# A mixer block in a newly searched order: convolution as fp32 products, head norm by columns, a kept row scale, two row maxima

## The chip, the core and the metric

One core of a Trainium2 chip runs the whole program. It has five engines with a queue each: TensorE (PE, with its weight loads shown as PEld), VectorE (DVE), ScalarE (ACT), GpSimd (POOL) and SyncE (SP), which issues transfers. The metric is the time of one execution on the device in microseconds, taken as the median of some runs.

## What is computed

The reference is one layer of an encoder with 512 rows of 1024 columns, in fp32. Three sublayers follow one another; each normalizes the rows, scales and shifts them by factors made from a second input, applies its function, normalizes the result and adds it, gated, to the running rows.

```python
def sublayer(h_res, j, fn, res_w):
    h = rms_norm(h_res, norm_g[l, 2 * j]) * (1.0 + scale) + shift
    y = rms_norm(fn(h), norm_g[l, 2 * j + 1])
    return h_res + res_w * gate * y
...
x = sublayer(x, 0, lambda h: swiglu(h, ffn1_w_in[l], ffn1_w_out[l]), 0.5)
x = sublayer(x, 1, mixer, 1.0)
x = sublayer(x, 2, lambda h: swiglu(h, ffn2_w_in[l], ffn2_w_out[l]), 0.5)
```

The change lies in the middle one. The mixer projects its 1024 columns to q, k, v, a recurrent branch xr and a gate branch yr, each 512 wide. q, k and v go through differential attention with four heads: two softmaxes per head, the second subtracted with a factor, then a norm over the head's 128 columns. xr goes through a convolution over time with four taps per channel, then through two recurrences, forward and backward, each with two gates; their sum is multiplied with GeLU of yr. Both halves are joined and projected.

```python
xc = lax.conv_general_dilated(xr, conv_w[:, None, :], window_strides=(1,), padding=[CONV_PAD],
        dimension_numbers=('NWC', 'WIO', 'NWC'), feature_group_count=D_LRU) + conv_b
h = rg_lru(xc, w_gate[0], b_gate[0], lam[0], False) + rg_lru(xc, w_gate[1], b_gate[1], lam[1], True)
...
p = jax.nn.softmax(s, axis=-1)
w = p[:, :, 0] - lam * p[:, :, 1]
...
o = rms_norm(o, subln_g) * (1.0 - lambda_init)
```

## The kernel before

Everything lies transposed: a tile has 128 channels on its partitions and the 512 rows along its free dimension, so X, the running rows, is eight such tiles. A large product is made in three fp32r products (mm3, L153 to L155): each factor is split into a high and a low part, and high x high, low x high and high x low are summed in PSUM. Weights come in units of up to 128x1024: SyncE loads one (wdma), ScalarE copies its high part (L182), VectorE or GpSimd subtracts to get the low part (L190). PSUM has eight banks of 128x512; bank() takes the one that was freed first.

The mixer (from about 405 to 630 us) is a list of small steps, MIXER, which a loop in mixer() runs through once while the program is built. Each name is a step and its argument: "sc.2" the scores of block 2. A suffix p puts it on GpSimd, d on VectorE. The list sets the order in which each engine's queue holds its instructions. Each engine works through its own queue in order; between engines, a step waits for the data and the buffers that it needs. The steps that the change and the prediction touch:

- kk, gm: the last units of the first seven column groups (four of xr, q and k of head 0, q of head 1), still on rows that are scaled but not normalized; sd, sr, rv: the norm (L994, L1001, L1004). xs, xa, rs, ra (L1041, L1049, L1106) then apply the norm to those groups.
- hm, hf, hh, hl (L1008 to L1019): the normalized columns, split high and low, for all later projections. pj: a projection, in two halves of four column tiles; vp: one of eight steps of v; vh, vl: v's parts.
- cv (L1269, L1273): the convolution of one of four groups of 128 channels on VectorE, one scaling and three multiply-adds with shifted columns; ch, cl (L1281, L959): its high and low part. ga: the two gates' products of one group and direction; gs (L1305): their sigmoids; le, lq, lr, lg, lm (L1312 to L1335): decay and input of the recurrence; ls (L1343): its scan; la (L1347), lf (L1366), lh, ll: sum of directions, times GeLU, split.
- rd, rp (L1122 to L1124): the rotary turn of q or k, three GpSimd operations; zA, zC (L1130, L1136): its split.
- sc (L1162): scores of one of 16 blocks (four heads, four blocks of 128 queries), both softmaxes side by side in two banks; mx (L1169): one operation takes the negated row maxima of both banks; ex (L1175): exponentials with row sums; wr, w1, w2 (L1180, L1184, L1188): the two softmaxes scaled and subtracted; tp, th, tl (L1199, L1209, L959): transposed and split.
- pv: weights times v; po: its copy and square; ms, me, sq, rc, mu (L1233, L1237, L1241, L1244, L1248): the norm over a head's columns, made as a full 128x512 tile: a product with ones that sums and spreads, times 1/128 plus epsilon, square root, reciprocal, product; ah, al (L1253, L1257): split.
- mo, mp: the output product, by unit of rows and by column tile; pf, pa (L1411, L1412, L1417): scaling and sum of squares for the norm that follows.

Around the mixer, X is kept with a row factor. When a sublayer's result F has its row norms s1 (a root of mean squares), half() and begin() set X to X x s1 + F (L418 to L422, L453) rather than dividing F. X is thus the true rows times s1, and the next norm's epsilon is scaled by s1 squared. To go on, the mixer divides X by it again: rr takes the reciprocal of s1 (L1425) and rx multiplies each of the eight tiles by it on GpSimd (L1428). last_tile() makes the last column tile of a result in two halves of 256 rows and the row norms after each (L899, L903, L904).

Of the kernel before, what the change touches and what calls it, by code (L numbers as in the profile page):

```python
# [81 lines left out]
ra.q2 vl.1 ex.3 wr.2 rd.q2 rx.3 lq.21 sc.0 ex.1 pj.k2a wr.3 w1.2 qkfree.0 mx.0 w1.3 ws.12 rx.6 wr.1 w2.2 ex.0
pj.k2b wl.12 w1.1 rxfree rp.q2 le.11 w2.1 wd.15 w2.3 sc.7 wr.0 ra.k2 lq.11 pj.q3a ws.13 rd.k2 mx.7 le.10 w1.0
wl.13 pj.q3b ex.7 w2.0 wd.16 lq.10 zA.q2 zC.q2 zF.q2 gs.30 sc.4 rp.k2 ga.31 mx.4 ws.14 gwfree tp.0 tp.2 wr.7 ra.q3 wl.14 tp.1
th.0 rd.q3 pj.k3a th.1 w1.7 zA.k2 th.2 lg.30 gs.31 w2.7 tl.2 zC.k2.p tp.3 tl.0 wd.17 sc.5 tl.1 th.3 sc.6
mx.5 ex.4 pj.k3b rp.q3 qkfree.1 zF.k2 tl.3 mx.6 ex.5 sc.9 wr.4 ra.k3 sc.8 wr.5 ex.6 mx.9 w1.4 rd.k3 sc.11 w1.5
pv.0 ws.15 w2.4 lg.31 w2.5 ex.9 wr.6 wl.15.p zA.q3 zC.q3 zF.q3 le.30 tp.4 tp.5 pj.y1a wr.9 w1.6 mx.8 wd.18 po.0 rp.k3 th.4
w2.6 ex.8 pj.y1b tl.4 mx.11 th.5 lr.10 tl.5 ms.0 w1.9 wr.8 lq.30 tp.7 w1.8 lr.11 w2.9 pj.y0a lm.10.p th.7 zA.k3
lr.30 w2.8 lr.21 lm.11.p tl.7 sc.10 ls.10 zC.k3.p yo.1 tp.6 ls.11 ex.11 qkfree.2 pj.y0b mx.10 lm.30 la.1
zF.k3 me.0 th.6 sc.14 ws.16 wr.11 lm.21.p tl.6 sc.15 mx.14 yo.0 pj.y2a wl.16.p ex.10 ls.21 ex.14 ls.30 wr.10 sc.12  # L90
w1.11 mx.15 wd.19 le.31 w1.10 sc.13 la.2 pv.1 wr.14 qkfree.3 mx.13 ex.15 w1.14 w2.11 ex.13 w2.14 tp.8 pj.y3a mx.12
# [1496 lines left out]
```

## Time and profile before

| | us |
|---|---|
| median of 3 runs (lowest, highest) | 1029.3 (1026.26, 1029.37) |
| the profiled execution | 1029.16 |
| its span, first to last instruction | 1027.0 |
| VectorE busy from 405 to 430 us | 24.97 of 25 |
| TensorE busy from 440 to 489 us | 38.80 of 49 |

The profile is of one execution. Its rows name an engine, the line of the kernel, the operation, output and inputs by the program's names (s and q are buffers of 128x512 and 128x4x512, PS is PSUM, wh and wl a weight's parts). An fp32r operand is shown as f32 for matmuls. Ends of matmuls are modelled and overlap; the time from one start to the next is what a matmul costs in a row of them.

### The profile page before, as it was taken

What the parts mean: (1) busy time and instruction counts of PE and PEld (TensorE: products, weight loads), DVE (VectorE), ACT (ScalarE), POOL (GpSimd) and SP (SyncE); (2) the same over time, 40 slices, a digit from 0 to 9 for tenths busy, and PEclk for the clock granted to TensorE, in tenths of its full rate; (3) what the DMA queues carried; (4) which work ended last, traced back from release to release, by engine and by line L of the source; (5) the groups of instructions that cost most, each with busy time, mean ns of one, the idle gap of its engine ahead of it and who ended that gap; (6) DMA issues with size and microseconds to landing.
All of it is one profiled execution on the core that took longest, in us unless ns stands there. A gap on an engine that the chain in (4) does not pass through costs nothing.

```text
span 1027.0 us, 11660 instructions
## 1 busy us (share of the span) xinstructions
PE 966.7 (94%) x4448; PEld 791.3 (77%) x4448; DVE 630.2 (61%) x730; ACT 429.4 (42%) x650; POOL 302.2 (29%) x218
## 2 busy tenths in 40 slices
PE   6999999999999998887888999989999999999994
PEld 4888888888888887665566788778888888888884
DVE  7967655556676649999788864887333333322226
ACT  6652233334222326566686953554322332222230
POOL 1008100000010136887887756562300000000114
PEclk9999999999999999988899999989999999999998
DMA  8745555554778642221220141223332233333312
GB/s 329 288 151 208 207 203 186 194 201 179 263 260 281 225 123 76 95 87 51 82 62 11 32 138 55 75 82 103 103 103 90 95 103 99 85 102 90 101 37 83
DMA packets 45002, 137.10 MB, mean 133 GB/s; under 512 B 7185, under 2 KB 9745, under 8 KB 44946
## 3 DMA queue, kind: packets, MB, share of 16 engines
q1 hardware_dynamic: 44082, 135.62, 39.9%
q8 instruction: 35, 0.57, 0.2%
q10 hardware_dynamic: 864, 0.74, 0.2%
q14 instruction: 21, 0.17, 0.0%
HBM read 132.14 MB, written 2.10 MB: 131 GB/s over the span
## 4 chain that ended last, share of the span: by engine, by line
PE 77%; DVE 15%; issue 3%; POOL 2%; ACT 2%; DMA 1%; SPq 0%; DVEq 0%; ACTq 0%; POOLq 0%
PE PS L154 25%; PE PS L153 25%; PE PS L155 25%; DVE wl L190 2%; DVE s L1273 2%; PE PS L1162 1%; DVE s L412 1%; DVE s L959 1%; PE PS L1199 1%; PE PS L700 1%; DVE sm L1169 1%; POOL s L524 1%; DMA q<-in_w_ada 1%; DVE X L453 1%; DVE X L422 1%
## 5 line engine op out<-in xcount | busy, mean ns | idle before, releaser
L153 PE MATMUL PS<-s,wh 128*128 128x512 f32 (+1 forms) x1032 | 397.2, 385 | 3.2 <-DVE sm L1169 1.7
L155 PE MATMUL PS<-s,wh 128*128 128x512 f32 (+1 forms) x1032 | 394.5, 382 | 5.7 <-DVE s L959 2.5
L154 PE MATMUL PS<-s,wl 128*128 128x512 f32 (+1 forms) x1032 | 394.3, 382 | 3.5 <-POOL wl L190 2.1
L190 DVE TENSOR_TENSOR wl<-st,wh 128x1024 fp32r<-128x1024 f32 (+2 forms) x149 | 192.6, 1295 | 216.8 <-ACT wh L182 216.7
L155 PEld LDWEIGHTS PS<-s,wh 128*128 128x128 f32 x1032 | 195.4, 189 | 44.5 <-DVE s L959 2.9
L153 PEld LDWEIGHTS PS<-s,wh 128*128 128x128 f32 x1032 | 195.3, 189 | 44.1 <-DVE sm L1169 2.1
L154 PEld LDWEIGHTS PS<-s,wl 128*128 128x128 f32 x1032 | 195.5, 189 | 41.4 <-POOL wl L190 2.4
L182 ACT ACTIVATE wh<-st 128x1024 fp32r<-128x1024 f32 (+2 forms) x170 | 169.9, 1001 | 130.6 <-PE PS L155 109.8
L877 POOL TENSOR_TENSOR s<-s,s 128x512 f32<-128x512 f32 x12 | 16.3, 1356 | 402.7 <-ACT s L873 402.7
L153 PE MATMUL PS<-q,wh 128*128 128x512 f32 (+1 forms) x288 | 106.9, 371 | 0.0
L154 PE MATMUL PS<-q,wl 128*128 128x512 f32 (+1 forms) x288 | 106.1, 368 | 0.0
L155 PE MATMUL PS<-q,wh 128*128 128x512 f32 (+1 forms) x288 | 106.1, 368 | 0.0
L235 DVE CUSTOM_DVE_ANT_0 q<-q,q 128x1024 bf16<-128x1024 f32 x72 | 89.8, 1247 | 0.1
L791 DVE TENSOR_TENSOR s<-s,PS 128x512 f32<-128x512 f32 x41 | 28.1, 686 | 63.9 <-PE PS L155 63.2
L786 ACT ACTIVATE s<-PS 128x512 f32<-128x512 f32 x40 | 23.9, 596 | 99.9 <-PE PS L155 99.8
L154 PEld LDWEIGHTS PS<-q,wl 128*128 128x128 f32 x288 | 54.2, 188 | 10.0 <-issue 0.2
L153 PEld LDWEIGHTS PS<-q,wh 128*128 128x128 f32 x288 | 54.3, 188 | 9.9 <-issue 0.2
L155 PEld LDWEIGHTS PS<-q,wh 128*128 128x128 f32 x288 | 54.2, 188 | 9.6
L748 ACT ACTIVATE q<-s 128x512 fp32r<-128x512 f32 x28 | 17.7, 632 | 95.9 <-DVE s L791 94.5
L190 POOL TENSOR_TENSOR wl<-st,wh 128x1024 fp32r<-128x1024 f32 (+2 forms) x20 | 41.6, 2082 | 33.6 <-ACT wh L182 32.1
L748 ACT ACTIVATE s<-s 128x512 fp32r<-128x512 f32 x16 | 10.1, 632 | 70.5 <-DVE s L791 70.5
L749 DVE TENSOR_TENSOR q<-s,q 128x512 fp32r<-128x512 f32 x28 | 22.2, 792 | 20.0 <-ACT q L748 20.0
(229 smaller groups left out, 1035.5 us busy)
## 6 DMA issues: line engine op xcount, KB each, us to landing
q<-in_w_ada SPq DMA_DIRECT2D x72, 512.0 KB, 3.8
st<-in_w2b SPq DMA_DIRECT2D x37, 512.0 KB, 3.3
st<-in_w1b SPq DMA_DIRECT2D x36, 512.0 KB, 4.5
st<-in_w1o SPq DMA_DIRECT2D x16, 512.0 KB, 4.5
st<-in_w2o SPq DMA_DIRECT2D x16, 512.0 KB, 3.6
st<-in_wma SPq DMA_DIRECT2D x16, 448.0 KB, 3.9
st<-in_w2a SPq DMA_DIRECT2D x16, 448.0 KB, 3.4
st<-in_wmb SPq DMA_DIRECT2D x9, 512.0 KB, 3.3
```

The lines of the kernel that those rows point to most:

```text
L153: PE.matmul(o, wh, ah, start=start, stop=False)
L154: PE.matmul(o, wl, ah, start=False, stop=False)
L155: PE.matmul(o, wh, al, start=False, stop=stop)
L182: ACT.activation(h[:, :n], staged[i][:, :n], AF.Copy)
L190: eng.tensor_tensor(out=l[:, :n], in0=st[:, :n], in1=h[:, :n].bitcast(F32), op=ALU.subtract)
L235: DVE.tensor_tensor_reduce(out=junk, in0=t, in1=cond, op0=ALU.mult, op1=ALU.add, scale=1.0, scalar=0.0, accum_out=ada[:, i:i + 1])
L748: ACT.activation(h, t, AF.Copy)
L749: DVE.tensor_tensor(out=l, in0=t, in1=f32(h), op=ALU.subtract)
L786: ACT.activation(t, PS[:, b], AF.Silu)
L791: DVE.tensor_tensor(out=g, in0=g, in1=PS[:, b], op=ALU.mult)
L877: POOL.tensor_tensor(out=st["acc"], in0=st["acc"], in1=t, op=ALU.add)
L1273: DVE.scalar_tensor_tensor(out=o[:, t0:t1], in0=XR[:, i, t0 + d:t1 + d], scalar=cw(q), in1=o[:, t0:t1], op0=ALU.mult, op1=ALU.add)
```

## The change

The step list is replaced by another, found by a new search over orders and engines, with new steps in it:

- Convolution: dd builds on ScalarE, for a group of channels, four diagonal 128x128 matrices with the taps, by scaling the identity with a column. cv is now four fp32 products on TensorE, of a diagonal matrix with the shifted columns, summed in one bank. ce adds the bias and copies the result on ScalarE; ch and cl read the bank directly.
- Head norm: ms takes the sums with four products that have two columns each, me is a square root of 128x8 numbers on ScalarE, rc the reciprocal of these. dx scales the identity with them, into four diagonal matrices; rb multiplies ones with these, which spreads the factors over a bank; mu multiplies with that bank on VectorE.
- X keeps its scale: rx is gone. last_tile() multiplies each half's new row norms with the old reciprocal (one VectorE operation of 128x256), and half() uses that product as X's factor.
- Two row maxima per block (mx), one for each bank, and the two banks of a block are no longer sorted.
- rp is cut into r1, r2 and r3, and r1 to r3, w1, lg, la and pa can be on either engine.

```diff
+            if "old" in st:
+                DVE.tensor_tensor(out=st["old"][:, c], in0=s1[:, c], in1=st["old"][:, c], op=ALU.mult)
...
-            b = sb[n] = sorted((bank(), bank()))
+            b = sb[n] = (bank(), bank())
...
-            a, b = sb[n]
-            DVE.tensor_reduce(out=sm[:, n, 0:2], in_=PS[:, a:b + 1:b - a], axis=AX.X, op=ALU.max, negate=True)
+            for m in range(2):
+                DVE.tensor_reduce(out=sm[:, n, m:m + 1], in_=PS[:, sb[n][m]], axis=AX.X, op=ALU.max, negate=True)
...
+            b = O["m", h] = bank()
+            for q in range(4):
+                PE.matmul(PS[:, b, 2 * q:2 * q + 2], O[h][1][:, q * 128:q * 128 + 128], ones[:, 0:2], start=True, stop=True)
...
+            ACT.activation(rm[:, h], PS[:, b, 0:8], AF.Sqrt, scale=1.0 / 128, bias=epsc[:, 0:1])
...
+            DVE.reciprocal(rm[:, h], rm[:, h])
...
+            for q in range(4):
+                ACT.activation(t[:, q * 128:q * 128 + 128], ident, AF.Copy, scale=rm[:, h, 2 * q:2 * q + 1])
...
-            DVE.reciprocal(O[h][1], O[h][1])
...
+            DVE.tensor_tensor(out=o, in0=o, in1=PS[:, b], op=ALU.mult)
...
+            for q in range(4):
+                ACT.activation(dg[i][:, q * 128:q * 128 + 128], ident, AF.Copy,
+                               scale=par[:, C_CW + 4 * q + i:C_CW + 4 * q + i + 1])
...
-            for q, d in ((0, -2), (1, -1), (3, 1)):
+            for q, d in ((2, 0), (0, -2), (1, -1), (3, 1)):
                 t0, t1 = max(0, -d), min(S, S - d)
-                DVE.scalar_tensor_tensor(out=o[:, t0:t1], in0=XR[:, i, t0 + d:t1 + d], scalar=cw(q), in1=o[:, t0:t1],
-                                         op0=ALU.mult, op1=ALU.add)
+                PE.matmul(PS[:, b, t0:t1], dg[i][:, q * 128:q * 128 + 128], XR[:, i, t0 + d:t1 + d],
+                          start=d == 0, stop=q == 3)
...
-        def rx(e, k):
-            POOL.tensor_tensor(out=X[:, k], in0=X[:, k], in1=s1, op=ALU.mult)
...
-            return lambda st, c: G.half(st["F"], st["s1"], c)
+            return lambda st, c: G.half(st["F"], st.get("old", st["s1"]), c)
```

Of the list itself, the place of the first score block shows how far it is turned over: before, all of v's steps stand ahead of sc.2; now it comes after the first half of the k projection.

```diff
-lg.10 lm.20 zF.k0 rsfree gs.21 ls.01 rx.0 wl.10 ga.11 ws.11 la.0 ls.20 pj.q2a wd.13 vh.0 wl.11 gs.11 lg.21 vl.0
-vh.2 wd.14 vh.3 lg.11 sc.2 vl.2 vh.1 vl.3 le.21 sc.3 rx.2 mx.2 sc.1 rx.5 pj.q2b mx.3 rx.4 ex.2 mx.1 rx.1 ga.30
+ga.21 lg.01 cl.3 zC.q0 zF.q0 gs.21 ga.11 zC.k0 zF.k0 hl.1.p gs.11 pj.k1a sc.2 mx.2 gs.10 hl.7.p ce.3 le.00
+lq.00 pj.k1b ws.7 lg.10.p sc.0 ex.2 vp.0a mx.0 r2.q1.p ra.k1 wl.6.p vp.1a wl.7 le.10 rd.k1 r2.k1 r1.k1 lq.10
```

Three places of the engines' queues follow, each before and after; new lines of the kernel have other numbers (L959 is L965, L1004 is L1010, L1008 is L1014). A number behind a buffer's letter tells one use from another.

VectorE at the mixer's start, before: s_2635 is s1, s_2849 the mixer's norm.

```order
L190 TENSOR_TENSOR wl<-st,wh 128x896 x2
L1425 RECIPROCAL s_2635<-s_2635 128x512
L994 SCALAR_TENSOR_TENSOR s_2849<-PS,s_2848 128x512
L959 TENSOR_TENSOR q_3054<-q_81,q_3053 128x1024
L1004 RECIPROCAL s_2849<-s_2849 128x512
L1008 TENSOR_TENSOR s_3144<-X,s_2849 128x512
L1008 TENSOR_TENSOR s_3146<-X,s_2849 128x512
L1008 TENSOR_TENSOR s_3153<-X,s_2849 128x512
```

And now:

```order
L193 TENSOR_TENSOR wl<-st,wh 128x896 x2
L1000 SCALAR_TENSOR_TENSOR s_2849<-PS,s_2848 128x512
L1010 RECIPROCAL s_2849<-s_2849 128x512
L193 TENSOR_TENSOR wl<-st,wh 128x896
L1014 TENSOR_TENSOR s_3094<-X,s_2849 128x512
L193 TENSOR_TENSOR wl<-st,wh 128x896
L1014 TENSOR_TENSOR s_3147<-X,s_2849 128x512
L1021 TENSOR_SCALAR s_3158<-s_3158,aA,ada 128x512
```

The reciprocal of s1 and the split of the gates' weights (q_3054) no longer stand between the two weight splits and the norm; the reciprocal comes 43 rows later.

TensorE behind the last product of the column groups (s_2982, s_2983), before; s_3176 and the others are normalized columns.

```order
L153 MATMUL PS<-s_2982,wh 128x512
L154 MATMUL PS<-s_2982,wl 128x512
L155 MATMUL PS<-s_2983,wh 128x512
L153 MATMUL PS<-s_3176,wh 128x512
L154 MATMUL PS<-s_3176,wl 128x512
L155 MATMUL PS<-s_3177,wh 128x512
L153 MATMUL PS<-s_3169,wh 128x512
L154 MATMUL PS<-s_3169,wl 128x512
L155 MATMUL PS<-s_3170,wh 128x512
L153 MATMUL PS<-s_3164,wh 128x512
L154 MATMUL PS<-s_3164,wl 128x512
L155 MATMUL PS<-s_3165,wh 128x512
```

And now, where L1302 is the convolution, q_3055 is xr, s_3153, s_3142 and s_3189 are the diagonal matrices, s_3253 and s_3254 the convolved group's parts, q_3053 the gates' weights.

```order
L1302 MATMUL PS<-q_3055,s_3153 128x512
L1302 MATMUL PS<-q_3055,s_3153 128x510
L1302 MATMUL PS<-q_3055,s_3153 128x511 x2
L156 MATMUL PS<-s_2982,wh 128x512
L157 MATMUL PS<-s_2982,wl 128x512
L158 MATMUL PS<-s_2983,wh 128x512
L1302 MATMUL PS<-q_3055,s_3142 128x512
L1302 MATMUL PS<-q_3055,s_3142 128x510
L1302 MATMUL PS<-q_3055,s_3142 128x511 x2
L1302 MATMUL PS<-q_3055,s_3189 128x512
L1302 MATMUL PS<-q_3055,s_3189 128x510
L1302 MATMUL PS<-q_3055,s_3189 128x511 x2
```

The first half of the k projection has left this place, and three of the four convolutions stand in it, of which one comes ahead of the last column group.

VectorE behind the first two convolutions, before: s_3325 is the third convolution, q_3052 q of head 0.

```order
L190 TENSOR_TENSOR wl<-st,wh 128x1024
L959 TENSOR_TENSOR s_3282<-s_3247,s_3281 128x512
L959 TENSOR_TENSOR s_3286<-s_3252,s_3285 128x512
L190 TENSOR_TENSOR wl<-st,wh 128x1024
L1041 TENSOR_TENSOR s_3321<-PS,s_2849 128x512
L1269 TENSOR_SCALAR s_3325<-q_3055,par 128x512
L1273 SCALAR_TENSOR_TENSOR s_3325<-q_3055,par,s_3325 128x510
L1273 SCALAR_TENSOR_TENSOR s_3325<-q_3055,par,s_3325 128x511 x2
L1136 SCALAR_TENSOR_TENSOR s_3366<-q_3052,s_3365 128x512
L959 TENSOR_TENSOR s_3370<-s_3325,s_3369 128x512
```

And now, behind the low part of the first group (L1321 is cl, L1132 and L1136 are two thirds of the rotary turn, L1366 is lg):

```order
L965 TENSOR_TENSOR s_3248<-s_3202,s_3247 128x512
L1132 TENSOR_TENSOR q_3052<-q_3052,sinT 128x512
L193 TENSOR_TENSOR wl<-st,wh 128x1024
L1321 SCALAR_TENSOR_TENSOR s_3240<-PS,par,s_3239 128x512
L1321 SCALAR_TENSOR_TENSOR s_3300<-PS,par,s_3299 128x512
L1136 TENSOR_TENSOR q_3052<-q_3052 128x512
L1021 TENSOR_SCALAR s_3234<-s_3234,aA,ada 128x512
L1136 TENSOR_TENSOR q_3052<-q_3052 128x512
L1366 TENSOR_TENSOR q_3288<-q_3288,s_3322 128x512
L965 TENSOR_TENSOR s_3225<-s_3147,s_3224 128x512
L1366 TENSOR_TENSOR q_3288<-q_3288,s_3282 128x512
L1366 TENSOR_TENSOR q_3306<-q_3306,s_3282 128x512
```

The convolution is gone from this place; rotary operations and lg, which GpSimd had, stand there, and behind these rows follow the low part of the fourth group, the splits of head 0's q and k, and the first row maxima.

More of the change, by code (lines that the diff above doesn't have):

```diff
@@ L82 @@
[L82 to L91, printed above, removed]
@@ L1118, in rd, with r1, r2, r3 @@
                 SP.dma_start(out=rot[32 * q:32 * q + 32], in_=t[32 * p:32 * p + 32])
-        def rp(e, key):
+        def r1(e, key):
             t, rot = rp_[key]
-            POOL.tensor_tensor(out=t, in0=t, in1=cosT, op=ALU.mult)
-            POOL.tensor_tensor(out=rot, in0=rot, in1=sinT, op=ALU.mult)
-            POOL.tensor_tensor(out=t, in0=t, in1=rot, op=ALU.add)
+            e.tensor_tensor(out=t, in0=t, in1=cosT, op=ALU.mult)
+        def r2(e, key):
+            t, rot = rp_[key]
+            e.tensor_tensor(out=rot, in0=rot, in1=sinT, op=ALU.mult)
+        def r3(e, key):
+            t, rot = rp_[key]
+            e.tensor_tensor(out=t, in0=t, in1=rot, op=ALU.add)
         def zA(e, key):
@@ L1183, in w1 @@
             p = P[n][1]
-            POOL.tensor_scalar(out=p, in0=p, scalar1=sm[:, n, 7:8], scalar2=lamc[:, 4:5], op0=ALU.mult, op1=ALU.mult)
+            e.tensor_scalar(out=p, in0=p, scalar1=sm[:, n, 7:8], scalar2=lamc[:, 4:5], op0=ALU.mult, op1=ALU.mult)
         def w2(e, n):
@@ L1264, in mixer, with dd, ce @@
         am = {}
[L1266 to L1274 removed]
+        dg, cb = {}, {}
+        def dd(e, i):
+            dg[i] = ar.s()
+            for q in range(4):
+                ACT.activation(dg[i][:, q * 128:q * 128 + 128], ident, AF.Copy,
+                               scale=par[:, C_CW + 4 * q + i:C_CW + 4 * q + i + 1])
+        def cv(e, i):
+            b = cb[i] = bank()
+            for q, d in ((2, 0), (0, -2), (1, -1), (3, 1)):
+                t0, t1 = max(0, -d), min(S, S - d)
+                PE.matmul(PS[:, b, t0:t1], dg[i][:, q * 128:q * 128 + 128], XR[:, i, t0 + d:t1 + d],
+                          start=d == 0, stop=q == 3)
+            ar.give(dg.pop(i))
+        def ce(e, i):
+            xc[i] = ar.s()
+            b = cb.pop(i)
+            ACT.activation(xc[i], PS[:, b], AF.Identity, bias=par[:, C_CB + i:C_CB + i + 1])
+            unbank(b)
         def xrfree(e):
@@ L1280, in ch @@
             xch[i] = (ar.s(F32R), ar.s(F32R))
-            ACT.activation(xch[i][0], xc[i], AF.Copy)
+            ACT.activation(xch[i][0], PS[:, cb[i]], AF.Identity, bias=par[:, C_CB + i:C_CB + i + 1])
         def cl(e, i):
-            low(e, xch[i][1], xc[i], xch[i][0])
+            b = cb[i]
+            DVE.scalar_tensor_tensor(out=xch[i][1], in0=PS[:, b], scalar=par[:, C_CB + i:C_CB + i + 1],
+                                     in1=f32(xch[i][0]), op0=ALU.add, op1=ALU.subtract)
         def ga(e, k):
@@ L1327, in lg @@
             g = RI[d, 1][:, i]
-            POOL.tensor_tensor(out=g, in0=g, in1=xc[i], op=ALU.mult)
+            e.tensor_tensor(out=g, in0=g, in1=xc[i], op=ALU.mult)
             if d == 1:
@@ L1346, in la @@
             o = RI[1, 1][:, i]
-            POOL.tensor_tensor(out=o, in0=o, in1=RI[0, 1][:, i], op=ALU.add)
+            e.tensor_tensor(out=o, in0=o, in1=RI[0, 1][:, i], op=ALU.add)
         def rifree(e):
@@ L1416, in pa @@
             t = sqs.pop(m)
-            POOL.tensor_tensor(out=st["acc"], in0=st["acc"], in1=t, op=ALU.add)
+            e.tensor_tensor(out=st["acc"], in0=st["acc"], in1=t, op=ALU.add)
             ar.give(t)
@@ L1452, in part @@
                 mm3(PS[:, b, c], w[0][:, o], w[1][:, o], a[0][:, c], a[1][:, c], k == 0, k == 7)
+        st["old"] = s1
         last_tile(1, st, part, 4, nxt, early)
@@ L1504, in trunk_kernel @@
         G.begin(st["F"], st["s1"])
+        ar.give(st["old"])
         G.rest(2)
```

71 lines of the change are left out of this document (40 added, 31 removed).

## Prediction

> **What bounds the kernel now.** I read the page first, for the engines' totals.
>
> ```profile
> span 1027.0 us, 11660 instructions
> PE 966.7 (94%) x4448; PEld 791.3 (77%) x4448; DVE 630.2 (61%) x730; ACT 429.4 (42%) x650; POOL 302.2 (29%) x218
> ```
>
> TensorE is busy 94% of the span, and the two SwiGLUs on either side of the mixer hardly ever let it wait. So only the mixer is open, from 405 us (the last weights before its norm) to 630 us (its last products). The windows of that stretch are the second view; columns: length, then busy time and instructions of PE, PEld, DVE, ACT and POOL, then the granted clock.
>
> ```profile
> 405.00:430.00 25.00, 22.42 (x95) 17.25 (x93) 24.97 (x19) 13.95 (x19) 20.78 (x11) 1.00 0.31 104
> 430.00:440.00 10.00, 4.75 (x15) 3.08 (x16) 9.82 (x10) 6.95 (x12) 8.71 (x7) 0.88 0.12 26
> 440.00:489.00 49.00, 38.80 (x152) 30.64 (x151) 48.75 (x33) 32.67 (x48) 40.08 (x24) 0.88 0.26 75
> 489.00:566.00 77.00, 65.71 (x314) 47.28 (x312) 62.55 (x69) 56.02 (x109) 61.30 (x44) 0.96 0.17 48
> 566.00:630.00 64.00, 63.99 (x297) 51.95 (x298) 40.33 (x37) 43.72 (x77) 42.46 (x30) 0.97 0.27 83
> ```
>
> From 405 to 489 VectorE is never free and TensorE stands still for 2.58 + 5.25 + 10.20 us. From 489 to 566 TensorE stands still for another 11.29 us, and from 566 it has no gap at all. That is 29.3 us of waits. The clock loses more: (1 - clock) x busy time is 0.57, 4.66, 2.63 and 1.92 us in the last four windows, 9.8 us. Waits and clock together are **39.1 us**: all that any order of the mixer can win while TensorE does the same work.
>
> Third, TensorE's timeline, for what the larger gaps wait on (the bracket is the gap and its releaser).
>
> ```profile
> 430.33 0.50 PE L155 MATMUL PS<-s,wh 128*128 128x512 f32 x1 [1.05 <-POOL s L959]
> 437.58 0.74 PE L153 MATMUL PS<-s,q 128*128 128x512 f32 x1 [4.69 <-ACT s L1281]
> 478.47 0.80 PE L155 MATMUL PS<-wl,s 128*128 128x512 f32 x1 [5.48 <-DVE wl L190]
> 491.95 1.82 PE L1162 MATMUL PS<-s,s 64*128 64x512 f32 x7 [1.57 <-DVE q L959]
> 494.67 1.64 PE L1162 MATMUL PS<-s,s 64*128 64x512 f32 x5 [0.90 <-DVE sm L1169]
> ```
>
> The first gap is the k projection waiting for a normed column. The second is the gates waiting for the convolution (L1281 splits its result, L1273 makes it); the third is V's product waiting for a weight split that stands in VectorE's queue; the last two are scores behind evictions and row maxima.
>
> Why VectorE is full is in its rows by line, min/median/max in ns:
>
> ```profile
> L959 DVE TENSOR_TENSOR s<-s,s x7: 679/1749/1781, 426.0 to 474.5; 128x512 fp32r<-128x512 f32 x7
> L959 DVE TENSOR_TENSOR q<-PS,q x20: 666/678/692, 491.2 to 587.5; 128x512 fp32r<-128x512 f32 x20
> L1273 DVE SCALAR_TENSOR_TENSOR s<-q,par,s x12: 750/1659/2778, 431.9 to 464.4; 128x511 f32<-128x511 f32 x8, 128x510 f32<-128x510 f32 x4
> L1428 POOL TENSOR_TENSOR X<-X,s x8: 1251/1276/1727, 474.0 to 503.7; 128x512 f32<-128x512 f32 x8
> ```
>
> An operation with both operands in SBUF takes 0.68 us alone and 1.75 us while POOL works, POOL's own goes from 1.28 to 1.73, and with one operand in PSUM nothing slows it. So each POOL operation that meets VectorE costs VectorE about 1.07 us. The other two large kinds that stay on VectorE, alone and, for the first, beside POOL:
>
> ```profile
> 480.02 2.30 DVE L190 TENSOR_TENSOR wl<-st,wh 128x1024 fp32r<-128x1024 f32 x1
> 608.42 1.23 DVE L190 TENSOR_TENSOR wl<-st,wh 128x1024 fp32r<-128x1024 f32 x1 [0.60 <-ACT wh L182]
> 482.25 1.21 DVE L1343 TENSOR_TENSOR_SCAN q<-q,q 128x512 f32<-128x512 f32 x1
> L1169 DVE TENSOR_REDUCE sm<-PS 128x2 f32<-128x1024 f32 x16 | 19.5, 1220 | 10.9 <-PE PS L1162 4.3 <-PE PS L155 3.3 <-ACT s L1175 2.7
> ```
>
> The split of 608.42 is VectorE's last large one in the mixer; the last line is the row maxima.
>
> **The change, part by part.** *Convolution on TensorE.* Removed from VectorE, with the four other large operations that the head norm loses:
>
> ```profile
> L1273 DVE SCALAR_TENSOR_TENSOR s<-q,par,s 128x511 f32<-128x511 f32 (+1 forms) x12 | 19.2, 1599 | 0.4
> L1269 DVE TENSOR_SCALAR s<-q,par 128x512 f32<-128x512 f32 x4 | 3.0, 750 | 0.0
> L1244 DVE RECIPROCAL s<-s 128x512 f32<-128x512 f32 x4 | 13.2, 3327 | 0.3 <-ACT s L1241 0.3
> L1237 DVE TENSOR_SCALAR s<-PS 128x512 f32<-128x512 f32 x4 | 2.7, 677 | 1.2 <-PE PS L1233 1.2
> ```
>
> 38.1 us leave VectorE. On TensorE 16 fp32 products appear. The trace has such products in the old head norm; start to start one takes 544.47 - 543.61 = 0.86 us (two instructions), where an fp32r product takes 0.23.
>
> ```profile
> 543.15 0.39 PE L154 MATMUL PS<-s,wl 128*128 128x512 f32 x1
> 543.38 0.39 PE L155 MATMUL PS<-s,wh 128*128 128x512 f32 x1
> 543.61 1.02 PE L1233 MATMUL PS<-s,ones 128*128 128x512 f32 x2
> 544.47 0.60 PE L1199 MATMUL PS<-ident,s 128*128 128x128 f32 x4
> 394.64 1.62 PE L395 MATMUL PS<-ones,s 128*128 128x2 f32 x14
> ```
>
> 16 x 0.86 = **13.8 us**, all on TensorE, which is the engine that ends last. Bounds: 0.23 x 16 = 3.7 us if they ran like fp32r; above, at half clock, twice 0.86, 27.5 us. I take 13.8, the same form's own row.
>
> *Head norm by columns.* Its full-width product stays (now it spreads the factor); 16 products with two columns are new, at 1.62 / 14 = 0.116 us: **+1.9 us** on TensorE. Six operations in a chain replace five, and at the last head TensorE has two slices of the output product (24 x 0.23 = 5.5 us) to work on meanwhile, so I give the latency nothing. Uncovered, it would gain at most the old reciprocal's 3.3 us, or lose at most the two new links, four scalings of 0.36 us (below) and a product of 0.86.
>
> *ScalarE* gets 32 scalings of 128x128 with a column, four more evictions and two more table loads.
>
> ```profile
> L1412 ACT ACTIVATE s<-PS,aG x7: 678/682/718, 608.8 to 627.1; 128x512 f32<-128x512 f32 x7
> L894 ACT ACTIVATE s<-PS,aG x6: 460/467/468, 372.8 to 1012.6; 128x256 f32<-128x256 f32 x6
> L1313 ACT ACT_TABLE_LOAD x2 | 2.6, 1283 | 0.0
> ```
>
> Carried on in a straight line, 128 columns take 0.467 - 0.215 / 2 = 0.36 us, so 32 take 11.5 us, with the rest about 15 us, onto 153 us of 225. That is hidden except between convolution and gates (below). *Two maxima per block* instead of one of 1.22 us cost VectorE 16 x 0.14 us more, by the 0.68 us of an operation on one bank of PSUM; in return the first exponential starts 0.6 us earlier. I call it even.
>
> *X keeps its scale.* Eight POOL operations (L1428, 10.9 us with the mean 1.38) go, and so does the need for the 3.34 us reciprocal to run first:
>
> ```profile
> 410.45 3.34 DVE L1425 RECIPROCAL s<-s 128x512 f32<-128x512 f32 x1
> 413.71 0.62 DVE L994 SCALAR_TENSOR_TENSOR s<-PS,s 128x512 f32<-128x512 f32 x1
> 414.25 2.41 DVE L959 TENSOR_TENSOR q<-q,q 128x1024 fp32r<-128x1024 f32 x1
> 416.59 3.34 DVE L1004 RECIPROCAL s<-s 128x512 f32<-128x512 f32 x1
> ```
>
> The mixer's own reciprocal (L1004) now follows the statistics directly: it ends at about 415.1 instead of 419.9, 4.8 us earlier. TensorE has products until 428 either way, so this buys nothing by itself, but the normed columns are ready in time. Against it, one 128x256 product on VectorE stands in each half of the last norm's chain:
>
> ```profile
> L420 DVE TENSOR_TENSOR X<-X,s x8: 426/693/968, 376.8 to 638.3; 128x256 f32<-128x256 f32 x8
> ```
>
> 0.43 us with POOL idle, which here waits for the same product; behind it in VectorE's queue stand the products on X and the next weights' activations, for which TensorE waits. That is 0.4 to 0.9 us for both halves, and I take **+0.7**.
>
> *The new order.* I follow the engines' orders from 428 us with the durations above. TensorE: first convolution at 427.8, two more until 438.9, two gate pairs until 441.7. The next pair waits for a split that stands behind three two-operand operations on VectorE (1.7, 1.7 and 2.2 us, from 437.5): it starts at 443.8, **2.1 us** lost. The fourth convolution and three pairs end at 453.2, half of the k projection at 455.9. Then the first score block needs head 0's k, seven such operations later on VectorE, at about 459: **3.1 us** lost. V's eight steps (12 x 0.23 each) and three more score blocks end at 487 us. Before, V ended at 489 with half a q projection (2.7 us) done and no score block; now four blocks (3.5 us) are done. The front thus keeps 2.6 us of waits for the statistics, 5.2 us of these two, and at the clock of 0.88 for some 10 us another 1.2: **9.0** of its 23.3 us.
>
> For the attention part (15.8 us of waits and clock now) the two quoted waits of 1.57 and 0.90 us and 1.4 us of slow clock behind them go, since those blocks now run beside V's products, and so does L1237's (0.76 us). Of the 11.2 us left I keep **7.0**: VectorE's load there hardly falls (twelve scalings and half of the rope come over from POOL, the reciprocals go), so by kind these waits stay.
>
> [...] After the waits of 1.57 and 0.90 us the chain shows products 0.43 us apart, half speed:
>
> ```profile
> 497.03 0.43 PE PS L154
> 497.46 0.43 PE PS L155
> ```
>
> [...]
>
> **The sum.** 39.1 - 13.8 - 1.9 - 9.0 - 7.0 = 7.4 us saved, 0.7 given back: 6.7. The profiled execution took 1029.16 us (span 1027.0 us and 2.2 around it), 0.1 below the median of 1029.3, so I forecast **1022.5 us**. Its own range: if the remaining 16 us of waits are off by 6 either way, 1016.5 to 1028.5. As a check from VectorE: from 437 us on it keeps 64 two-operand operations at 0.65, eight scans and ten splits at 1.2, and some 49 us of the rest, 111 us; POOL's 52 operations add 1.07 each if all of them meet it (55 us), 33 if six in ten do. 144 us at the share that it reached before (152.5 us busy of 172.6 up to its last split) take 163 us: VectorE is done at 600, and 21.5 us later, as now, the mixer at 622. The first sum says 623.
>
> **The rivals.** *TensorE becomes the only bound.* The waits vanish but for the first 2.6: 39.1 - 15.7 - 2.6 - 0.7 = 20.1, so 1009; with a few left, 1012. For it speaks the last window, 64 us without a gap; against it, that two engines would be over 85% busy and hand work to each other. Chance 0.20.
>
> *The waits move.* The gate pairs need PSUM banks that only ScalarE's sigmoids free, and V's fourth bank comes from the first exponential; by my count that ends at 463.1 and V starts at 463.5. ScalarE has some 60 instructions between 416 and 455 there, 16 of 0.36 and the rest of about L1412's 0.68 us, 35 us in all. Should it run 7 us late, V starts 7 us late and the gain is gone: 1029. Chance 0.12. What speaks for it: its queue holds evictions behind copies that wait for VectorE, in order.
>
> *Slower: VectorE is slowed by POOL throughout.* The moved operations are two-operand ones. If nearly all of POOL's 52 operations meet them (45 to 55 us instead of 33), VectorE needs 156 to 166 us, 177 to 189 at its share, is done at 614 to 626, and the mixer ends at 636 to 647: 1035 to 1046. It decides from about 40 us of collisions. For it: L959's median of 1.75 us, near its maximum; against: fewer POOL operations are left to collide. Chance 0.13, at 1036.
>
> That the convolution wouldn't move can be left out: the order shows its products on TensorE.
>
> **How the numbers follow.** 0.55 for the forecast, 0.20, 0.12 and 0.13 for the rivals. Some 0.3% (3.1 us) is what a measurement of this kernel can tell from no change, so faster is below 1026. The forecast's own range lies nine tenths below it, 0.50, and the first rival adds 0.20, with a small part of the second: 0.72. Same: 0.05 and most of the second, 0.14. Slower 0.14. The range leaves out the far end of either rival: 1009 to 1032.
>
> **What would show it.** Right: the granted clock near 0.95 or more from 430 to 489; the fp32 products 0.86 us apart; TensorE's gaps at the third gate pair and at the first score block on VectorE, 2 and 3 us; V finished near 487; gaps of about 7 us afterwards. Wrong: two-operand operations on VectorE whose median stays at 1.7 us; a gap ahead of V that ends with an exponential or a sigmoid; fp32 products dearer than 0.86 us, which all falls on the end.

## The result and the profile after

The changed kernel took 1011.34 us (median of 4 runs, 1010.0 to 1013.34), the kernel before 1028.08 us beside it: ratio 0.984, 95% interval 0.9814 to 0.9866. That is 16.7 us less, where 6.7 were forecast; direction and range held, the size was off by 10. The profiled execution took 1012.05 us, 17.1 less than the profiled one of before. Its page:

```profile
span 1010.1 us, 11805 instructions
PE 973.8 (96%) x4512; PEld 796.6 (79%) x4512; DVE 598.1 (59%) x766; ACT 440.9 (44%) x687; POOL 238.9 (24%) x173
```

TensorE has more to do (973.8 us for 966.7) and the program is shorter. The mixer as one window shows why. Its last norm's first product comes at 611.72 us, where it came at 629.99. Columns: length, then busy time of PE, PEld, DVE, ACT and POOL, then the clock. First before, then after:

```profile
405.00:630.00 225.00, 195.67 (x868) 150.19 (x867) 186.42 (x164) 153.30 (x261) 173.33 (x113) 0.95 0.23 69
```

```profile
405.00:612.00 207.00, 201.61 (x932) 153.89 (x931) 155.71 (x198) 164.85 (x298) 110.14 (x68) 1.00 0.24 75
```

TensorE's waits fall from 29.3 to 5.4 us and its granted clock goes from 0.95 to 1.00. The work can be checked here: 195.67, less the 9.8 us that the slow clock had taken, plus 13.8 for the convolution and 1.9 for the head norm, is 201.6, as measured. GpSimd has 63 us less to do, VectorE 31. By stage, after:

```profile
428.00:440.00 12.00, 12.00 (x33) 5.93 (x33) 7.90 (x10) 10.30 (x17) 7.49 (x5) 1.00 0.36 101
440.00:487.00 47.00, 45.21 (x196) 33.40 (x195) 37.15 (x42) 44.53 (x72) 30.11 (x18) 1.00 0.27 87
487.00:550.00 63.00, 61.26 (x319) 49.03 (x317) 57.73 (x85) 53.06 (x99) 33.59 (x21) 1.00 0.22 67
550.00:612.00 62.00, 62.00 (x302) 49.00 (x301) 32.52 (x50) 42.55 (x85) 21.94 (x16) 1.00 0.27 81
612.00:645.00 33.00, 29.10 (x171) 25.17 (x170) 27.70 (x31) 15.28 (x26) 21.59 (x19) 0.95 0.14 42
```

TensorE is the only bound now, although VectorE is busy 57.7 of 63 us beside it in the third row. All waits of TensorE of 0.4 us or more that are left up to 620 us, in its timeline after, with the convolutions (L1302), the first score block (L1174) and the start of the last norm (L902):

```profile
407.61 1.12 PE L472 MATMUL PS<-s,ones 128*128 128x512 f32 x2 [1.85 <-POOL s L468]
...
427.84 3.59 PE L1302 MATMUL PS<-q,s 128*128 128x512 f32 x8
431.96 7.01 PE L1302 MATMUL PS<-q,s 128*128 128x512 f32 x16
443.39 0.50 PE L158 MATMUL PS<-s,q 128*128 128x512 f32 x1 [1.23 <-DVE s L1321]
445.17 3.69 PE L1302 MATMUL PS<-q,s 128*128 128x512 f32 x8 [0.56 <-ACT q L1343]
455.60 0.96 PE L1174 MATMUL PS<-s,s 64*128 64x512 f32 x6
...
493.24 0.50 PE L156 MATMUL PS<-s,wh 128*128 128x512 f32 x1 [0.46 <-ACT s L1116]
503.21 0.50 PE L156 MATMUL PS<-s,wh 128*128 128x512 f32 x1 [1.28 <-DVE q L965]
...
611.72 0.59 PE L902 MATMUL PS<-s,ones 128*128 128x256 f32 x2
616.51 0.39 PE L156 MATMUL PS<-s,wh 128*128 128x256 f32 x1 [1.21 <-ACT s L412]
617.70 0.39 PE L158 MATMUL PS<-s,wh 128*128 128x256 f32 x1 [0.69 <-DVE s L415]
```

The first score block starts without a wait at 455.6; the forecast had it behind 3.1 us of waiting, at 459. Its reason is on VectorE, in the rows that lead to that block:

```profile
446.93 1.76 DVE L1136 TENSOR_TENSOR q<-q 128x512 f32<-128x512 f32 x1
448.62 0.68 DVE L1366 TENSOR_TENSOR q<-q,s 128x512 f32<-128x512 f32 x1
449.22 0.68 DVE L965 TENSOR_TENSOR s<-s,s 128x512 fp32r<-128x512 f32 x1
...
453.78 0.68 DVE L965 TENSOR_TENSOR s<-q,s 128x512 fp32r<-128x512 f32 x1
```

From 448 us on they take 0.68 us, since GpSimd waits just there, for ScalarE (L1025, and L1343 after that):

```profile
443.77 4.37 POOL L965 TENSOR_TENSOR s<-s,s 128x512 fp32r<-128x512 f32 x3
450.76 1.29 POOL L965 TENSOR_TENSOR s<-s,s 128x512 fp32r<-128x512 f32 x1 [2.62 <-ACT s L1025]
455.90 1.29 POOL L1366 TENSOR_TENSOR q<-q,s 128x512 f32<-128x512 f32 x1 [3.85 <-ACT q L1343]
```

### The profile page after: what moved, and what is told of

Same layout as the page of the kernel before. It is cut to its first block, busy times and chain, and to the rows that moved or that the text cites. A ratio compares the mean times of both kernels' runs of the same rounds, so it can differ in the third digit from the quotient of the medians.

```text
span 1010.1 us, 11805 instructions
## 1 busy us (share of the span) xinstructions
PE 973.8 (96%) x4512; PEld 796.6 (79%) x4512; DVE 598.1 (59%) x766; ACT 440.9 (44%) x687; POOL 238.9 (24%) x173
## 4 chain that ended last, share of the span: by engine, by line
PE 86%; DVE 6%; ACT 3%; POOL 2%; issue 2%; DMA 1%; SPq 1%; DVEq 0%; ACTq 0%; POOLq 0%
PE PS L156 27%; PE PS L157 27%; PE PS L158 27%; PE PS L1174 1%; DVE wl L193 1%; DVE s L415 1%; PE PS L703 1%; PE PS L1211 1%; POOL s L527 1%; DVE X L456 1%; DVE X L425 1%; DMA q<-in_w_ada 1%; DVE s L1549 1%; POOL s L468 1%; DVE X L423 1%
## 5 line engine op out<-in xcount | busy, mean ns | idle before, releaser
L193 DVE TENSOR_TENSOR wl<-st,wh 128x1024 fp32r<-128x1024 f32 (+3 forms) x150 | 190.5, 1272 | 226.7 <-ACT wh L185 226.6
L156 PEld LDWEIGHTS PS<-q,wh 128*128 128x128 f32 x288 | 54.3, 189 | 10.2 <-issue 0.6
L193 POOL TENSOR_TENSOR wl<-st,wh 128x1024 fp32r<-128x1024 f32 (+1 forms) x19 | 38.4, 2020 | 55.3 <-ACT wh L185 50.4
```

Of the source, the lines that this page charges most:

```text
L156: PE.matmul(o, wh, ah, start=start, stop=False)
L193: eng.tensor_tensor(out=l[:, :n], in0=st[:, :n], in1=h[:, :n].bitcast(F32), op=ALU.subtract)
```

## Experiments

Two questions: which bound the changed kernel has, and where the forecast's waits went. All ratios are to the kernel before on the same chip, which took 1026.3 to 1027.2 us there; the changed kernel stands at 0.984, some 1010 us. A price below is the difference of two ratios times 1027 us, good to about 3 us. In the profiled executions some of that lies ahead of every edit: the mixer's first wait ends between 407.6 and 409.3 us. Most of these kernels have the step list on one line, so their lines are numbered 29 or 30 lower: L936 or L935 is L965, L1145 is L1174, L1273 is L1302.

**All four convolutions back on VectorE**, in the new list:

```diff
+            if i in {0, 1, 2, 3}:
+                o = xc[i] = ar.s()
...
+                for q, d in ((0, -2), (1, -1), (3, 1)):
+                    t0, t1 = max(0, -d), min(S, S - d)
+                    DVE.scalar_tensor_tensor(out=o[:, t0:t1], in0=XR[:, i, t0 + d:t1 + d], scalar=cw(q), in1=o[:, t0:t1],
+                                             op0=ALU.mult, op1=ALU.add)
+                return
```

> The changed kernel with all four convolutions back on VectorE, at the same places of the new list (no diagonal matrices, no fp32 products, the bias in VectorE's first scaling; the split reads SBUF again). TensorE loses 13.8 us of products, VectorE gets back some 22 us (19.2 + 3.0 by the rows of before) between 428 and 450 us. Theory relief (the waits went because VectorE lost work; the products are cheaper than the waits that they remove): the gates wait for VectorE again, 4 to 6 us a group at first, and the time is 1013 to 1025 us in spite of 13.8 us less on TensorE. Theory order (the new list removes the waits by itself, the move of the convolution is a cost): 998 to 1003 us.

1025.07 us, ratio 0.9989 (0.9977 to 1.0001): the whole gain is gone. TensorE in its front:

```profile
446.06 0.80 PE L156 MATMUL PS<-s,q 128*128 128x512 f32 x1 [15.82 <-ACT s L1331]
455.59 0.80 PE L158 MATMUL PS<-s,q 128*128 128x512 f32 x1 [4.16 <-DVE s L965]
466.59 0.50 PE L156 MATMUL PS<-s,wh 128*128 128x512 f32 x1 [3.48 <-ACT q L1362]
```

It has 13.8 us less to do and stands still for 23.5; its clock of 0.71 from 428 to 440 us and 0.78 from there to 487 costs another 8.0. The relief of VectorE in the front is what this order lives on.

**One convolution back on VectorE**, the fourth group's, by the same edit for that group:

> The changed kernel with only the last convolution (group 3) on VectorE, which has some 10 of 47 us free there now. If TensorE alone is the bound: 3.4 us less, 1008 us. If VectorE's front is as full as the prediction had it: the first score block waits 3 to 6 us longer for head 0's split, and the time is 1011 to 1015 us.

1014.78 us, 0.9886 (0.9871 to 0.9901), 4.7 us more. The time is as the second theory had it, but the wait stands at another place: at the gates' products, ahead of the first score block. L1331 is ScalarE's copy of the convolved group, L1362 the gates' sigmoids:

```profile
452.74 0.63 ACT L1331 ACTIVATE s<-s 128x512 fp32r<-128x512 f32 x1 [3.94 <-DVE s L1307]
455.03 0.80 PE L156 MATMUL PS<-s,q 128*128 128x512 f32 x1 [5.11 <-ACT q L1362]
```

VectorE isn't full: it is busy 36.0 us from 440 to 487, and the convolution's four operations take 2.9. It is done late (452.7 us), since it stands behind other work in VectorE's queue; ScalarE's sigmoids stand behind its copy, and TensorE behind them.

**Each convolution made twice** on TensorE:

```diff
-            for q, d in ((2, 0), (0, -2), (1, -1), (3, 1)):
+            for _ in range(2):
+                for q, d in ((2, 0), (0, -2), (1, -1), (3, 1)):
...
```

> The changed kernel with each convolution made twice into the same bank (the second pass overwrites the first): 16 more fp32 products, 13.8 us more on TensorE and nothing else. If TensorE alone bounds the mixer now: 12 to 14 us more, 1023.5 to 1025.5. If VectorE or ScalarE hold the front as well, part of it disappears in waits that were there: less than 10 us more, under 1021.

1021.42 us, 0.9953 (0.9939 to 0.9968): 16 products more cost 11.6 us of their 13.8, and of the waits of 1.23 and 0.56 us behind them 0.25 is left. TensorE is the bound: what it gets to do falls on the end, less the small waits that it fills.

**The new steps in the old list**, on the engines that the old steps had, each put where its old step stood (the convolution right ahead of its split); one piece of the list:

```diff
-wl.5 hh.6 hl.4.p ch.2 ga.01 gs.00 hl.6 wd.8 cl.2 rp.q0 pj.k1b wl.6 gs.01 rs.q1 wd.9
+wl.5 hh.6 hl.4.p cv.2 ch.2 cl.2 ce.2 ga.01 gs.00 hl.6 wd.8 r1.q0.p r2.q0.p r3.q0.p pj.k1b wl.6 gs.01 rs.q1 wd.9
```

> The new steps (convolution on TensorE, head norm by columns, two maxima, kept scale with its late reciprocal) in the list of before, with each new step put beside the one that it belongs to and the old engines kept for the rope, w1, lg, la and pa. Theory relief: most of the gain without the new list, 1012 to 1019 us. Theory order: the new steps alone only add 15.7 us to TensorE in a list that was made for others, 1026 to 1036 us.

1026.8 us, 0.9995 (0.9986 to 1.0005): without its order, and with the rotary, softmax and gate operations left on GpSimd that the change moves to VectorE, it gains nothing. From 440 us on the front is nearly free here (a wait of 2.56 us stands ahead, at 437), and the attention isn't:

```profile
440.00:487.00 47.00, 45.41 (x175) 32.62 (x174) 22.89 (x23) 36.22 (x53) 31.30 (x22) 0.99 0.29 86
487.00:550.00 63.00, 57.33 (x281) 42.26 (x280) 54.94 (x69) 51.11 (x97) 46.11 (x33) 0.95 0.18 51
550.00:612.00 62.00, 58.30 (x274) 45.42 (x275) 32.71 (x50) 49.21 (x96) 36.86 (x27) 1.00 0.21 68
```

From 487 to 550 VectorE is busy 54.9 us, less than the 57.7 of the changed kernel, and TensorE still waits 5.7 us where that one waits 1.7. So VectorE's load alone doesn't make these waits. GpSimd is busier here, though, 46.1 us for 33.6; the next run keeps its load and has the new list.

**Each of the other steps undone alone**, in the new list. GpSimd gets all rotary products, w1, lg and la back, 28 operations (suffix p in the list):

> The changed kernel with every rope third, w1, lg and la on GpSimd, as before (28 operations go back from VectorE, places in the list unchanged). VectorE loses some 18 us of its own work; GpSimd gets some 36 us. Theory collisions (the attention part lost its waits because GpSimd has fewer operations that stall VectorE's, and because GpSimd's own chain is short): 3 to 10 us slower than the changed kernel, ratio 0.987 to 0.994. Theory relief (what counts is the work that VectorE lost): the same or faster, ratio 0.982 to 0.985.

1019.37 us, 0.9928 (0.9913 to 0.9943), 9.0 us more. Its attention:

```profile
487.00:550.00 63.00, 59.95 (x294) 45.92 (x293) 52.37 (x67) 50.91 (x94) 47.19 (x34) 1.00 0.24 71
```

With GpSimd busy 47.2 us TensorE waits 3.1 us in this window, between the 5.7 of the old list and the 1.7 of the changed kernel. The same new steps on these engines are 6.9 us faster in the new list than in the old one (some other operations change engine with the list). So the list counts by itself, and so do the moves from GpSimd to VectorE. The head norm as a full tile again, with VectorE's reciprocal of 128x512:

> The changed kernel with the head norm made on the full tile as before (one product, 1/128 plus epsilon on VectorE, root on ScalarE, reciprocal of 128x512 on VectorE, product on VectorE; the list's other steps unchanged). TensorE loses 1.9 us, VectorE gets 16 us between 540 and 605 us. Theory TensorE alone is the bound there, with the heads' chains hidden: 1 to 2 us faster, ratio 0.982. Theory VectorE's relief counts there too: 2 to 6 us slower, ratio 0.986 to 0.990.

1026.04 us, 0.9999 (0.9982 to 1.0015). One row maximum for both banks, on sorted banks:

> The changed kernel with one operation for both row maxima of a block and sorted banks. VectorE gets 16 x 0.14 us less; each block's first exponential starts 0.6 us later. By the prediction (even): within 1 us, ratio 0.983 to 0.985. If the first exponential's start and the banks that it frees matter: 2 to 5 us slower, ratio 0.986 to 0.989.

1020.26 us, 0.9945 (0.9924 to 0.9966). X divided again on GpSimd (rx at every tenth step behind rr):

> The changed kernel with X divided by its scale again: eight GpSimd products, one after every tenth step behind the reciprocal, which stays late; the two products of row norms in the last half norms go. By the prediction's terms: 0.9 us less in the last norm's chain, eight more collisions of 1.07 us on VectorE, which now has room: within 1.5 us, ratio 0.983 to 0.986. If GpSimd's queue is as tight as before: 3 to 6 us slower, ratio 0.987 to 0.990.

1023.31 us, 0.9964 (0.9954 to 0.9974). The last three cost 16.3, 10.8 and 12.7 us, more than either side had expected: the idea that a step is worth what its operations cost fell. Each undone step opens waits in its own stretch. With the full-tile norm, in the stretch where VectorE has the large reciprocals again:

```profile
566.58 0.80 PE L158 MATMUL PS<-q,q 128*128 128x512 f32 x1 [2.63 <-DVE q L965]
...
604.75 0.50 PE L157 MATMUL PS<-q,wl 128*128 128x512 f32 x1 [2.92 <-DVE wl L193]
```

**All old steps in the new list**, to close the square of list and steps: the five undone together.

> All old steps in the new list: convolution on VectorE, full-tile head norm, one row maximum per block, rotary and gate products on GpSimd, X divided again. It closes the square of list and steps (the new steps in the old list took 0.9995 of the kernel before). Theory 1, list and steps only fit each other: slower than before, ratio 1.005 to 1.025, with TensorE's waits spread over the whole mixer. Theory 2, the list itself carries part of the gain: 0.990 to 0.997.

1067.69 us, 1.0388 (1.0363 to 1.0413): slower than expected by either theory, on the first one's side. The prices of the five alone sum to 64 us; together they cost 56. Old list and old steps 1, new list and old steps 1.0388, both new 0.984; the old list with four of the five new steps 0.9995, and the new list with the same four 0.9928. The four gain nothing without the list, and the list loses without the steps. The fifth, the moves from GpSimd to VectorE, wasn't run in the old list.

**The kept scale alone in the old list**, with its reciprocal late:

```diff
-        def rx(e, k):
-            POOL.tensor_tensor(out=X[:, k], in0=X[:, k], in1=s1, op=ALU.mult)
...
+            if "old" in st:
+                DVE.tensor_tensor(out=st["old"][:, c], in0=s1[:, c], in1=st["old"][:, c], op=ALU.mult)
```

> The kernel before with the kept scale alone: the eight GpSimd products on X go, the reciprocal comes later, and the product with the old reciprocal stands in each half of the last norm; the rest of the old list is untouched. By the prediction's terms it buys nothing ahead of 428 us and gives back 0.7 us at the end: ratio 0.999 to 1.002. Rival: GpSimd's eight products at 474 to 504 us slow VectorE's splits and evictions there by 1.07 us each and TensorE waits for those, so it gains 3 to 6 us: 0.994 to 0.997.

1027.44 us, 1.0016 (1.0002 to 1.0029): 1.6 us slower, as its 0.7 us at the end and no gain ahead of it would have it. In the new list its undoing cost 12.7.

**GpSimd kept busy where it waited in the front.** This is the test of the forecast's failed step: five products into a buffer that nobody reads fill GpSimd's waits of 2.62 and 3.85 us.

```diff
+        def nz(e, n):
+            for _ in range(n):
+                POOL.tensor_tensor(out=noise, in0=cosT, in1=sinT, op=ALU.mult)
...
-ga.21 lg.01 cl.3 zC.q0 zF.q0 gs.21 ga.11 zC.k0 zF.k0 hl.1.p gs.11 pj.k1a sc.2 mx.2 gs.10 hl.7.p ce.3 le.00
-lq.00 pj.k1b ws.7 lg.10.p sc.0 ex.2 vp.0a mx.0 r2.q1.p ra.k1 wl.6.p vp.1a wl.7 le.10 rd.k1 r2.k1 r1.k1 lq.10
+ga.21 lg.01 cl.3 zC.q0 zF.q0 gs.21 ga.11 zC.k0 zF.k0 hl.1.p gs.11 pj.k1a sc.2 mx.2 gs.10 nz.2 hl.7.p ce.3 le.00
+lq.00 pj.k1b ws.7 nz.3 lg.10.p sc.0 ex.2 vp.0a mx.0 r2.q1.p ra.k1 wl.6.p vp.1a wl.7 le.10 rd.k1 r2.k1 r1.k1 lq.10
```

> The changed kernel with five more GpSimd products of 128x512, into a buffer that nobody reads, at the two places where GpSimd waits between 448 and 456 us (2.6 and 3.9 us). Theory 1, the collisions that the prediction counted are absent there only because GpSimd stands still: VectorE's two-operand operations of 448 to 454 us go from 0.68 back to 1.6 to 1.75 us, the first score block comes at 458 to 461 us instead of 455.6, with a gap of 2 to 5 us on TensorE, and the time rises by 2 to 5 us: ratio 0.986 to 0.989. Theory 2, VectorE has slack there: VectorE slows, TensorE has other work, less than 1 us: 0.9835 to 0.985.

1014.43 us, 0.988 (0.9865 to 0.9895), 4.1 us more. VectorE's same operations and the first score block:

```profile
448.85 1.77 DVE L1337 TENSOR_TENSOR q<-q,s 128x512 f32<-128x512 f32 x1
450.55 1.79 DVE L936 TENSOR_TENSOR s<-s,s 128x512 fp32r<-128x512 f32 x1
...
457.35 1.75 DVE L936 TENSOR_TENSOR s<-q,s 128x512 fp32r<-128x512 f32 x1
```

```profile
455.84 0.50 PE L1145 MATMUL PS<-s,s 64*128 64x512 f32 x2
459.15 1.22 PE L1145 MATMUL PS<-s,s 64*128 64x512 f32 x4 [2.81 <-DVE s L936]
```

The first two products of the block start early, and the others wait for the low part of k. The forecast's wait is back, at its place (459) and near its size (2.8 for 3.1 us). So is some slow clock, 0.93 from 440 to 487 us. **Memsets in the same places**, fifteen of 128x512 at 0.57 us (of full size, unlike the wording below), which read nothing:

> The same two places of GpSimd's queue, filled with 15 memsets of a quarter of the size instead of the five products, so that GpSimd is as busy but reads nothing. It tells a delay of GpSimd's own queue from a slowing of VectorE. If the cost of the run with products comes from two engines reading SBUF together, this one is even with the changed kernel (0.983 to 0.985) and VectorE's operations stay near 0.68 us; if it comes from GpSimd's queue being late, both cost the same.

1012.8 us, 0.9864 (0.9849 to 0.9879). The two medians differ by 1.6 us and their intervals overlap; the rows tell the cases apart. VectorE beside the memsets (448.72 to 452.16 and 454.31 to 459.51):

```profile
449.25 0.68 DVE L1337 TENSOR_TENSOR q<-q,s 128x512 f32<-128x512 f32 x1
449.85 0.68 DVE L936 TENSOR_TENSOR s<-s,s 128x512 fp32r<-128x512 f32 x1
456.10 0.68 DVE L936 TENSOR_TENSOR s<-q,s 128x512 fp32r<-128x512 f32 x1
```

No slowing, and no wait ahead of the scores. This run was expected even and isn't quite (2.5 us by the ratios, within their error; 0.7 by the two spans). In the profiled execution the fourth convolution, ahead of the scores, takes 5.09 us instead of 3.69.

**The same for the attention**, twelve such products in GpSimd's five longest waits between 488 and 535 us (nz.4 ahead of r2.q2, nz.2 ahead of w1.4, zC.k2, wl.15 and lm.20):

> The changed kernel with twelve more GpSimd products of 128x512, into a buffer that nobody reads, at the five places where GpSimd waits between 488 and 535 us (7.7, 3.1, 3.0, 4.0 and 3.8 us). Theory 1, the attention's waits are absent because VectorE meets GpSimd less often there: VectorE's two-operand operations slow by about 1.07 us each, and with only 5.3 of 63 us free it can't take 5 to 10 us more, so TensorE's waits come back, 4 to 7 us: ratio 0.988 to 0.991. Theory 2, the new order gives TensorE other work at each such place: under 2 us, 0.984 to 0.986.

1021.0 us, 0.9939 (0.9927 to 0.995), 10.2 us more, above what either theory gave. Its window and TensorE's new waits:

```profile
487.00:550.00 63.00, 55.67 (x258) 42.41 (x257) 61.37 (x71) 48.24 (x89) 48.85 (x30) 0.92 0.19 59
```

```profile
506.37 2.24 PE L1145 MATMUL PS<-s,s 64*128 64x512 f32 x6 [3.35 <-DVE q L936]
510.03 0.80 PE L126 MATMUL PS<-s,wh 128*128 128x512 f32 x1 [1.41 <-DVE q L936]
...
538.80 1.32 PE L1182 MATMUL PS<-ident,s 128*128 128x128 f32 x8 [2.09 <-ACT s L1158]
```

VectorE is busy longer (61.4 us) with fewer instructions done (71 for 85). **Load on VectorE instead**, eight products beside the softmax subtractions:

> The changed kernel with eight more VectorE products of 128x512, into a buffer that nobody reads, one behind or ahead of each of eight softmax subtractions between 492 and 543 us, where VectorE is busy 57.7 of 63 us: 5.4 us more alone, up to 14 beside GpSimd. Theory 1, VectorE's load decides whether TensorE waits there: 4 to 8 us more, 0.988 to 0.992. Theory 2, the order has slack (VectorE's results are needed later than they come): under 2 us, 0.984 to 0.986.

1016.39 us, 0.9896 (0.9877 to 0.9915): 5.8 us more for 6.5 us of work. The group of the added products, and the window:

```profile
L1438 DVE TENSOR_TENSOR noise<-cosT,sinT 128x512 f32<-128x512 f32 x8 | 6.5, 818 | 0.0
```

```profile
487.00:550.00 63.00, 58.65 (x287) 46.33 (x286) 61.20 (x82) 51.20 (x94) 31.86 (x19) 0.97 0.19 59
```

In that window TensorE lost 61.26 - 58.65 = 2.6 us to waits and 0.03 x 58.65 = 1.8 to the clock; the rest of this profiled execution's loss lies in the front, whose fourth convolution took 6.53 us. So about two thirds of the added work fall on the end: VectorE has little slack there, although TensorE hardly waits for it. By the same reckoning the twelve products cost 5.6 us of waits and 4.5 of clock in this window, as much as their whole 10.2.

## Why the prediction was off, point by point

**What bounds the kernel.** Right: 39.1 us of waits and clock were what could be won. Of these 5.4 are left, and 0.0 of clock: 39.1 - 15.7 - 5.4 = 18.0. The last norm's first product came 18.3 us earlier; from there to the end the changed kernel takes 1.4 us longer (398.4 for 397.0), which leaves the 16.9 us between the spans.

**Work on TensorE.** Right. Sixteen fp32 instructions take 7.01 us in a row, the last one 0.59 of it:

```profile
L1302 PE MATMUL PS<-q,s x32: 590/592/697, 427.8 to 448.3; 128*128 128x511 f32 x16, 128*128 128x512 f32 x8, 128*128 128x510 f32 x8
```

(7.01 - 0.59) / 15 = 0.428 apart, two to a product: 0.86, as forecast. The sum over the mixer fits to 0.1 us. ScalarE's scalings and the head norm's chain cost nothing that shows: none of the listed waits ends with them, and from 550 to 612 us TensorE is busy 62.00 of 62.

**The kept scale.** Right: the product is 0.42 us (L910), and TensorE's wait behind it went from 0.76 to 1.21 us. The rest of the 1.4 goes with the clock of 0.95 from 612 us on. In the memsets' run, which has the same products and the same wait, that clock is 1.00, so it isn't a price of the kept scale alone.

**Two row maxima, called even.** Right in its own cost, since the rows stay at 0.68 us, but wrong as a part of this order: with one maximum, on sorted banks, the kernel loses 10.8 us.

**The front, 9.0 us kept.** This is one of the two steps that failed; 3.6 were left (1.85, 1.23 and 0.56). Of the 5.4 between, 3.1 are the wait ahead of the first score block and 1.2 the slow clock that was kept; the small waits make the rest (1.85 for 2.6, 1.23 for 2.1, and 0.56 that wasn't foreseen). Place and order were right: the third gate pair waited (443.39 for 443.8), and V's products followed. What failed is "the first score block needs head 0's k, seven such operations later on VectorE, at about 459": the seven were priced beside GpSimd, which stood still. When GpSimd was made busy there, 459 and 2.8 us came out.

**The attention, 7.0 us kept.** The other failed step; 1.7 were left. "VectorE's load there hardly falls" was so (57.7 of 63 us), but "so by kind these waits stay" doesn't follow. With the new steps and GpSimd's old load, the old list keeps 5.7 us of waits in that window and the new one 3.1; with GpSimd relieved as well, 1.7. So the list removed the larger part and the moves from GpSimd the rest (the windows are equal in time, not step by step). Added work brings waits back: 5.6 us with twelve products on GpSimd, 2.6 with eight on VectorE itself. Which of the list's many shifts took away which wait wasn't tested.

**The check from VectorE** hid the same mistake. It had 144 us of VectorE's work from 437 us, with 33 of collisions; the changed kernel's VectorE is busy 129.6 us from 437 to 612:

```profile
437.00:612.00 175.00, 171.46 (x821) 133.17 (x820) 129.59 (x178) 141.84 (x256) 86.67 (x54) 1.00 0.26 81
```

At its share before (152.3 of 172.6 us by the trace; the forecast has 152.5) that is 147 us, to 584, and the mixer would end 21.5 us later, at 605, ahead of TensorE's own 612. (The 21.5 run from that split's start; from its end, to which the 172.6 go, it is 20.3.) By its own rule, with the measured load, the forecast would have chosen its first rival, "TensorE becomes the only bound" (1009 to 1012, chance 0.20), which came. "Six in ten" of GpSimd's operations was a guess, and its sensitivity wasn't followed: 14 us on VectorE decide between the two cases.

**The other rivals.** ScalarE hardly ran late: one wait, of 0.56 us, ends with a sigmoid (L1343), at the fourth convolution, and between that and V's products there is none of 0.3 us. The slower one, VectorE slowed throughout, didn't come, but GpSimd's products did slow it where they were put beside it: 1.75 to 1.79 us for 0.68 in the front, and twelve of them added to the attention cost 10.2 us.

**The slow clock.** The forecast kept some of it, 1.2 us in the front; in the kernel before, products stood 0.43 us apart after waits of 1.57 and 0.90 us. The changed kernel lost none up to 612 us: its granted clock is 1.00 from 405 us to there. In the rows of three runs the length of a wait doesn't tell whether the products behind it slow. After 1.23 and 0.56 us, in the changed kernel, eight convolution instructions took 3.69 us; after 1.37 and 1.47 us, with one row maximum, 6.49:

```profile
444.52 0.50 PE L158 MATMUL PS<-s,q 128*128 128x512 f32 x1 [1.37 <-DVE s L1321]
447.19 6.49 PE L1302 MATMUL PS<-q,s 128*128 128x512 f32 x8 [1.47 <-ACT q L1343]
```

and with the full-tile norm, after 1.36 and 1.51 us, 3.69 again:

```profile
444.91 0.50 PE L158 MATMUL PS<-s,q 128*128 128x512 f32 x1 [1.36 <-DVE s L1316]
447.61 3.69 PE L1297 MATMUL PS<-q,s 128*128 128x512 f32 x8 [1.51 <-ACT q L1338]
```

So nearly equal waits stand ahead of 6.49 us in one execution and of 3.69 in the other; what decides between them, no run shows. These rows also tell how finely the runs can be read: up to 2.8 us of a single execution's time can be this one place (6.49 for 3.69), whatever the edit.

**What stays open.** How much of the 10.2 us of the twelve products is VectorE's slowing and how much GpSimd's own lateness wasn't separated. Nor is it shown that the undone steps cost as much in a list searched for them; each was put at a place chosen by hand. And the moves from GpSimd to VectorE weren't tried without the new list.
